# Gate products written to PSUM in their copy's order, 64 first products ahead, eight rows' dot products at the seam

## The chip, the cores and the metric

The kernel runs on 1 core of one Trainium2 chip, as one launch. The metric is the device time of that launch in microseconds (us). TensorE is called PE here, its weight loads PEld, VectorE DVE, ScalarE ACT, GpSimd POOL, and SyncE SP.

## The reference

Three transformer-like layers over 512 tokens of width 1024, in float32. The part that the change touches most is the mixture with 16384 experts in the first layer:

```python
q = (nf @ w_q).reshape(t, PEER_HEADS, D_KEY)
...
v1, i1 = lax.top_k(s1, TOPK)
v2, i2 = lax.top_k(s2, TOPK)
cand = (v1[..., :, None] + v2[..., None, :]).reshape(t, PEER_HEADS, TOPK * TOPK)
vals, ci = lax.top_k(cand, TOPK)
...
idx = (e1 * N_KEYS + e2).reshape(t, PEER_HEADS * TOPK)
gates = jax.nn.softmax(vals.astype(jnp.float32), axis=-1).astype(n.dtype)
...
ug = expert_u[ib]
act = jax.nn.gelu(jnp.einsum("td,tkd->tk", xb, ug)) * gb
vg = expert_v[ib]
return jnp.einsum("tk,tkd->td", act, vg)
```

Each token takes 8 heads x 16 experts. Ahead of it stands a mixing layer (gated convolutions with a normalization per head, spatial gating), behind it a state-space layer, an attention layer and two feed-forward layers, each with normalizations and matrix products.

## The kernel before

Activations lie feature by partition, 8 tiles of 128 x 512. A weight matrix is read in strips of 128 output features; every strip (`wr`) is split into a rounded part `wh` (ACT) and a remainder `wl` (DVE, or POOL where the strip's `pool` flag is set), and each product is three matmuls for each 128 inputs: `wh` by the rounded activation, `wl` by it, `wh` by its remainder (lines 161 to 163). `lin` is one strip's product. `lin2` takes the first two strips behind a normalization together: all but the last input tile of the one, then of the other, then the last tile of both.

The code writes every engine's instructions in the order in which that engine runs them. Small steps of a chain (a normalization, a convolution) are put into a heap by `later(n, f)` and come out n products later; a list `bg` of background steps with costs is drawn from after each product, by a credit.

The experts are done in two ways. The first 128 tokens gather their experts' rows, which are multiplied and summed on DVE and POOL's queue (`first_block`: a row's dot product is line 980, its gather line 977). The other 384 tokens go dense: for each of 128 groups e of 128 experts a first product (`u`, 24 matmuls of 384 columns), a Gelu, a multiplication with the gates `G`, and 18 matmuls of 512 columns into six PSUM banks (`pv`, line 1112).

The gates stage comes ahead of the dense stage. `plan_choice` finds the 16 best candidates of a token and head, ending in `ints` and `trans`: `trans` turns expert numbers and gates with three PE transposes (`pt`, lines 867 to 869). `plan_gates` makes from them a gate for every token and expert: `front` builds one-hot tables for 8 tokens (`oh2` and `oh1`, then `gh`, four of the eight on ACT, line 906, four on DVE, line 908), `mid` multiplies them on PE (`pg`, line 917, four tokens to a PSUM bank), and `back` copies each bank on ACT into `gb` (line 924), which goes to DRAM (`gd`) and comes back in the dense stage as `G`. `gb` holds, for each of 128 experts, 32 tokens side by side:

```python
pg = self.px_((P, 4, P), "pg")
...
    nc.tensor.matmul(pg[:, t % 4, :], oh2[:, t, :], gh[:, t, :], start=True, stop=True)
...
copy(gb[:, c % 2, :, o : o + 4].rearrange("p e t -> p t e"), pg)
```

While this goes on, PE runs first products of groups that need no gates yet: `R` = 56 of the 128 are done ahead, their Gelus are kept in DRAM (`sd`), and the dense stage reads them back. `bg` also holds 32 early rows' dot products (`EARLY`) of the first 128 tokens. The costs of `bg` are spread evenly over the first products of this stage.

## Time and profile before

| what | value |
|---|---|
| median of 3 runs | 3077.76 us (3073.26 to 3085.12) |
| profiled execution, its own time | 3078.27 us |
| span of the profiled execution | 3076.5 us |
| mean granted TensorE clock | 0.971 |
| PE busy | 2908.9 us, 95% |
| DVE busy | 2218.9 us, 72% |
| ACT busy | 1303.4 us, 42% |
| POOL busy | 1093.8 us, 36% |

The time is that of the launch, and the span runs from its first to its last instruction. Busy matmuls overlap at their ends, so that a busy PE is not a PE at its peak. The granted clock is a share of full speed; 1.0 is 2.4 GHz and the lower level is 1.2 GHz, and a share between is a stretch that had both.

### The profile page before, as it was taken

Reading aid. Unit: us, or ns where it says so; the run is one execution under the profiler, and the core shown is the slowest. Engines: PE = TensorE matmul, PEld = TensorE weight load, DVE = VectorE, ACT = ScalarE, POOL = GpSimd, SP = SyncE. Lnnn points to the kernel's source line nnn. Section 1 sums busy time; section 2 is a strip of 40 time slices with the busy share of each in tenths; the row PEclk is TensorE's granted clock in tenths of the full one; section 3 lists DMA queues with packets and bytes.
Section 4 is the critical chain, followed back from the end, with each engine's and each line's share of the span. In section 5 each row is a group of like instructions: output and inputs, shape, how many; then the busy total and the mean of one; then the engine's idle time right before and its main releaser. Section 6 shows DMA issues by size and latency. Waiting matters only on the chain. (4 is left out here: it accounts for less than half of the span.)

```text
span 3076.5 us, 39413 instructions
## 1 busy us (share of the span) xinstructions
PE 2908.9 (95%) x14359; PEld 2445.6 (79%) x14359; DVE 2218.9 (72%) x3788; ACT 1303.4 (42%) x2209; POOL 1093.8 (36%) x936
## 2 busy tenths in 40 slices
PE   8999988889999999999999979999999998999998
PEld 6677888788887888888787768888877766888886
DVE  7945888986888889988886674666666356566665
ACT  4333246566433433443335343433344345433333
POOL 3224566653248778877872321000011011100001
PEclk9889999899999999999999989999999989999999
DMA  4124335679778988898894473233332211333323
GB/s 140 48 83 148 97 129 186 232 245 313 252 263 313 336 318 322 331 350 315 312 328 147 125 225 103 77 102 99 99 97 95 77 42 42 96 103 96 96 72 99
DMA packets 235067, 534.77 MB, mean 174 GB/s; under 512 B 35135, under 2 KB 127683, under 8 KB 222202
## 3 DMA queue, kind: packets, MB, share of 16 engines
q1 hardware_dynamic: 170570, 343.69, 33.9%
q0 software_dynamic: 24832, 140.74, 12.4%
q10 hardware_dynamic: 39472, 47.84, 4.5%
q8 instruction: 113, 1.85, 0.2%
q14 instruction: 80, 0.66, 0.1%
HBM read 468.75 MB, written 63.44 MB: 173 GB/s over the span
## 5 line engine op out<-in xcount | busy, mean ns | idle before, releaser
L150 DVE TENSOR_TENSOR wl<-wr,wh 128x1024 fp32r<-128x1024 f32 (+2 forms) x453 | 545.3, 1213 | 510.1 <-ACT wh L148 509.9
L148 ACT ACTIVATE wh<-wr 128x1024 fp32r<-128x1024 f32 (+2 forms) x552 | 544.7, 995 | 403.7 <-PE mm L163 196.2
L161 PE MATMUL mm<-xn,wh 128*128 128x512 f32 x1296 | 520.9, 402 | 14.3 <-ACT xn L119 8.9
L163 PE MATMUL mm<-xn,wh 128*128 128x512 f32 x1296 | 512.4, 395 | 5.8 <-DVE xn L114 5.8
L162 PE MATMUL mm<-xn,wl 128*128 128x512 f32 x1296 | 512.1, 395 | 1.9 <-POOL wl L150 1.9
L230 POOL TENSOR_TENSOR accs<-accs,sq 128x512 f32<-128x512 f32 x56 | 86.3, 1541 | 1042.7 <-ACT sq L229 1038.4
L1112 PE MATMUL pv<-wh,A 128*128 128x512 f32 x1536 | 437.5, 397 | 15.8 <-ACT A L117 5.9
L150 POOL TENSOR_TENSOR wl<-wr,wh 128x1024 fp32r<-128x1024 f32 x99 | 241.3, 2439 | 449.1 <-ACT wh L148 446.6
L161 PE MATMUL mm<-n,wh 128*128 128x384 f32 x1024 | 350.6, 342 | 0.8 <-ACT gs L705 0.8
L162 PE MATMUL mm<-n,wl 128*128 128x384 f32 x1024 | 345.6, 337 | 5.9 <-DVE wl L150 4.3
L1112 PEld LDWEIGHTS pv<-wh,A 128*128 128x128 f32 x1536 | 286.8, 189 | 80.6 <-DVE A L112 11.0
L163 PE MATMUL mm<-n,wh 128*128 128x384 f32 x1024 | 345.9, 338 | 3.1 <-DVE n L114 3.1
L161 PEld LDWEIGHTS mm<-xn,wh 128*128 128x128 f32 x1296 | 248.5, 192 | 69.3 <-ACT xn L119 8.9
L163 PEld LDWEIGHTS mm<-xn,wh 128*128 128x128 f32 x1296 | 247.7, 191 | 61.4 <-DVE xn L114 8.3
L162 PEld LDWEIGHTS mm<-xn,wl 128*128 128x128 f32 x1296 | 248.4, 192 | 55.2 <-POOL wl L150 2.3
L1112 PE MATMUL pv<-wl,A 128*128 128x512 f32 x768 | 241.9, 396 | 9.4 <-DVE wl L150 9.3
L117 ACT ACTIVATE A<-ga 128x384 fp32r<-128x384 f32 x128 | 67.3, 526 | 357.7 <-DVE ga L1076 357.7
L162 PEld LDWEIGHTS mm<-n,wl 128*128 128x128 f32 x1024 | 194.2, 190 | 9.7 <-DVE wl L150 5.6
L161 PEld LDWEIGHTS mm<-n,wh 128*128 128x128 f32 x1024 | 194.5, 190 | 4.9 <-issue 1.4
L163 PEld LDWEIGHTS mm<-n,wh 128*128 128x128 f32 x1024 | 194.0, 189 | 3.4 <-DVE n L114 3.4
L1112 PEld LDWEIGHTS pv<-wl,A 128*128 128x128 f32 x768 | 144.0, 189 | 49.0 <-DVE wl L150 17.3
L1670 ACT ACTIVATE uc<-up,vec 128x512 f32<-128x512 f32 x88 | 71.8, 816 | 203.8 <-DVE up L1668 203.8
(414 smaller groups left out, 5438.9 us busy)
## 6 DMA issues: line engine op xcount, KB each, us to landing
wr<-in_exp_u SPq DMA_DIRECT2D x128, 512.0 KB, 5.4
wr<-in_exp_v SPq DMA_DIRECT2D x128, 512.0 KB, 6.9
wr<-in_w_up SPq DMA_DIRECT2D x88, 512.0 KB, 3.6
gd<-gb ACTq DMA_DIRECT2D x48, 512.0 KB, 5.0
G<-gd SPq DMA_DIRECT2D x32, 768.0 KB, 6.3
wr<-in_w_dn SPq DMA_DIRECT2D x64, 320.0 KB, 2.9
wr<-in_w_pg SPq DMA_DIRECT2D x24, 512.0 KB, 4.2
sd<-gs SPq DMA_DIRECT2D x56, 192.0 KB, 2.9
```

Source lines behind the costliest of these rows:

```text
L117: nc.scalar.activation(hi, src, AF.Copy)
L148: nc.scalar.activation(s.hi, s.raw, AF.Copy)
L150: eng.tensor_tensor(s.lo, s.raw, s.hi.bitcast(F32), ALU.subtract)
L161: t.matmul(ps, wh, xh, start=start, stop=False)
L162: t.matmul(ps, wl, xh, start=False, stop=False)
L163: t.matmul(ps, wh, xl, start=False, stop=stop)
L230: self.later(1, lambda: nc.gpsimd.tensor_tensor(acc, acc, sq, ALU.add))
L1112: nc.tensor.matmul(pv[2 * b + h], a[:, x, o], w[:, h * T : h * T + T], start=(e == 0 and i == 0 and w is s.hi), stop=last)
L1670: nc.scalar.activation(c, u, AF.Identity, scale=w(2), bias=cb[:, m : m + 1])
```

## The change

- The gate products' PSUM tile is laid out expert by token (`P, P, 4`): each product writes every fourth element, and the copy reads the bank straight and writes runs of four elements. `oh1` is laid out token by token, and DVE's `gh` compares with the copy of the iota that lies in PSUM (`iotaP`).
- `R` goes from 56 to 64: eight more first products run in the gates stage, eight fewer in the dense stage.
- `TAIL`: the last 8 of the 32 early rows' dot products are taken out of the mix and put behind the last gate copy.
- `trans` is drawn from `bg` a few steps after `ints`; the other steps of a block of tokens are spread over one product fewer.
- The dense stage's Gelu writes back into its PSUM bank, and the gate multiplication reads it there.
- `lin2` always goes back and forth between its two strips.
- In the mixing layer, two steps of the head normalization come out a product later.
- The attention bias's small loads are issued earlier, and a negation goes from POOL to DVE.

```diff
-        if first:
-            for k in range(n + 1):
-                for i, j in ((0, k), (1, k - 2)):
-                    if 0 <= j < n - 1:
-                        self.prod(pss[i], ss[i], rhs, j, j + 1)
-        else:
-            for s, ps in zip(ss, pss):
-                self.prod(ps, s, rhs, 0, n - 1)
+        for k in range(n + 1):
+            for i, j in ((0, k), (1, k - 2)):
+                if 0 <= j < n - 1:
+                    self.prod(pss[i], ss[i], rhs, j, j + 1)
...
-            self.later(1, lambda: self.two_rms(d["sq"], self.sel2, 1.0, scale))
+            self.later(1, lambda: self.two_rms(d["sq"], self.sel2, 1.0, scale, 2))
...
-        self.later(1, turn)
+        self.later(lag, turn)
...
-                    self.later(1, lambda: self.head_ln(acc, lambda yn: ln_a(j, yn)))
+                    self.later(2, lambda: self.head_ln(acc, lambda yn: ln_a(j, yn)))
...
-    R = 56
+    R = 64
...
+    TAIL = 8
...
-        self.bg = self.bias_prep() + [(0.1, lambda: nc.scalar.copy(iotaP, iota))]
+        bias, loads = self.bias_prep()
+        loads()
+
+        self.bg = [(0.1, lambda: nc.scalar.copy(iotaP, iota))] + bias
...
-                oh1 = self.loc((P, P, A), BF16, tag="oh1", bufs=2)
+                oh1 = self.loc((P, A, P), BF16, tag="oh1", bufs=2)
...
-                    nc.scalar.activation(gh[:, t, :], oh1[:, :, t], AF.Copy, scale=g)
+                    nc.scalar.activation(gh[:, t, :], oh1[:, t, :], AF.Copy, scale=g)
                 else:
-                    nc.vector.tensor_scalar(out=gh[:, t, :], in0=iota, scalar1=e1, scalar2=g, op0=ALU.is_equal, op1=ALU.mult)
+                    nc.vector.tensor_scalar(out=gh[:, t, :], in0=iotaP, scalar1=e1, scalar2=g, op0=ALU.is_equal, op1=ALU.mult)
...
-                pg = self.px_((P, 4, P), "pg")
+                pg = self.px_((P, P, 4), "pg")
...
-                    nc.tensor.matmul(pg[:, t % 4, :], oh2[:, t, :], gh[:, t, :], start=True, stop=True)
+                    nc.tensor.matmul(pg[:, :, t % 4], oh2[:, t, :], gh[:, t, :], start=True, stop=True)
...
-                copy(gb[:, c % 2, :, o : o + 4].rearrange("p e t -> p t e"), pg)
+                copy(gb[:, c % 2, :, o : o + 4], pg)
...
-        bg = part(1, 1)
...
+        turn = {0: part(1, 1), 1: nxt[1], 2: nxt[2]}
+        turn = {b: (x, x.pop())[1] for b, x in turn.items()}
+        bg = part(1, 1)[:-1] + nxt[1][:3] + [turn[0]]
+        nxt[1] = nxt[1][3:]
...
+        rows, last = rows[: self.EARLY - self.TAIL], rows[self.EARLY - self.TAIL :]
...
-                m = -(-len(more) // (k - j))
+                m = -(-len(more) // max(1, k - 1 - j))
...
-        bg += [(0.0, lambda: mid(n - 1)), (0.0, lambda: back(n - 2)), (0.0, lambda: back(n - 1)), (0.0, rest)]
+            if b in turn:
+                bg.append(turn[b])
+        bg += [(0.0, lambda: mid(n - 1)), (0.0, lambda: back(n - 2)), (0.0, lambda: back(n - 1)), (0.0, rest)] + last
...
-                s = self.tmp((P, TD), tag="gs")
-                nc.scalar.activation(s, ps, AF.Gelu_apprx_tanh)
-                gated(e, s)
+                nc.scalar.activation(ps, ps, AF.Gelu_apprx_tanh)
+                gated(e, ps)
...
-            nc.gpsimd.tensor_scalar(out=rb[0:32, :], in0=rb[0:32, :], scalar1=-1.0, scalar2=None, op0=ALU.mult)
...
+        def negate():
+            nc.vector.tensor_scalar(out=rb[0:32, :], in0=rb[0:32, :], scalar1=-1.0, scalar2=None, op0=ALU.mult)
```

Where the gates stage meets the dense stage, these rows stood on DVE: the last two of 32 dot products (`x,first`, line 980) between the last one-hot tables, then the remainders (`wl`) of the strips that come next, and then the first gate multiplication (`ga`).

```order
L980 SCALAR_TENSOR_TENSOR x,first<-x,accs 128x1024
L894 TENSOR_TENSOR oh_1085_6364<-e2T_2397,held_1484 128x1024
L902 TENSOR_TENSOR oh_1087_6367<-e1T_2396,held_1484 128x512
L908 TENSOR_SCALAR gh_6366<-iota_1482,e1T_2396,gT_2398 128x128 x4
L980 SCALAR_TENSOR_TENSOR x,first<-x,accs 128x1024
L150 TENSOR_TENSOR wl_6410<-wr_6258,wh_6409 128x1024
L150 TENSOR_TENSOR wl_6484<-wr_6319,wh_6483 128x1024
L150 TENSOR_TENSOR wl_6515<-wr_6413,wh_6514 128x1024
L1076 TENSOR_TENSOR ga_6547<-gs_6545,G_6475 128x384
L112 TENSOR_TENSOR A_6549<-ga_6547,A_6549 128x384
```

With the change the last table is followed by all of the last eight dot products (now line 989, five and three), with one remainder between them, and then by the same remainders and the first gate multiplication, which now reads the Gelu from its product's own tile.

```order
L902 TENSOR_TENSOR oh_1117_6559<-e1T_2396,held_1484 128x512
L908 TENSOR_SCALAR gh_6558<-held_1484,e1T_2396,gT_2398 128x128 x4
L989 SCALAR_TENSOR_TENSOR x,first<-x,accs 128x1024 x5
L150 TENSOR_TENSOR wl_6645<-wr_6512,wh_6644 128x1024
L989 SCALAR_TENSOR_TENSOR x,first<-x,accs 128x1024 x3
L150 TENSOR_TENSOR wl_6682<-wr_6606,wh_6681 128x1024
L150 TENSOR_TENSOR wl_6756<-wr_6648,wh_6755 128x1024
L150 TENSOR_TENSOR wl_6789<-wr_6685,wh_6788 128x1024
L1085 TENSOR_TENSOR ga_6820<-mm_6761,G_6747 128x384
L112 TENSOR_TENSOR A_6822<-ga_6820,A_6822 128x384
L150 TENSOR_TENSOR wl_6826<-wr_6759,wh_6825 128x1024
```

On DVE, eight dot products have thus moved from between the tables to behind the last of them and in front of the first `ga`. On PE, in the mixing layer, this is where the second convolution's accumulator (`cacc`) enters its head normalization: behind two `psb` products, which end the two chains before it, and right ahead of a projection's strip (`mm`, of which the last and the first matmul stand here).

```order
L163 MATMUL mm_766<-xn_103,wh_626 128x512
L381 MATMUL psb_791<-rT_737,selT 128x512
L381 MATMUL psb_796<-rT_744,selT 128x512
L339 MATMUL pmn_810<-cacc_460,bd_87 128x512
L161 MATMUL mm_825<-xn_103,wh_701 128x512
```

With the change it stands one strip later, behind a transpose of a chain's statistics (`pst`).

```order
L163 MATMUL mm_805<-xn_103,wh_682 128x512
L370 MATMUL pst_830<-ident,rl_112_729 4x128 x4
L335 MATMUL pmn_837<-cacc_460,bd_87 128x512
L377 MATMUL psb_839<-rT_782,selT 128x512
L357 MATMUL psv_844<-sel_91,sq_785 128x2 x4
```

The `pmn` product has moved past the 24 matmuls of one strip, and the `psv` and `pst` steps of the chains with it.

## Rows read from the trace of the kernel before

**Rows 1.** The page's first part: busy time, share of the span and instructions, by engine.
```profile
PE 2908.9 (95%) x14359; PEld 2445.6 (79%) x14359; DVE 2218.9 (72%) x3788; ACT 1303.4 (42%) x2209; POOL 1093.8 (36%) x936
```
**Rows 2.** Gates stage, dense stage: us, busy PE, PEld, DVE, ACT, POOL, clock, DMA share, GB/s.
```profile
395.00:761.50 366.50, 313.04 (x1953) 305.54 (x1951) 314.52 (x726) 231.13 (x407) 210.17 (x159) 0.94 0.63 216
761.50:1651.00 889.50, 860.04 (x4164) 740.93 (x4165) 754.26 (x956) 349.13 (x629) 598.53 (x572) 0.99 0.86 309
```
**Rows 3.** PE's waits over the span: us in total, times, longest.
```profile
PE pg L917 <- ACT gb L924: 30.9, 20, 6.3
PE pt L867 <- DVE ef L863: 10.2, 2, 6.4
PE pv L1112 <- DVE wl L150: 9.3, 14, 1.5
...
PE pmn L339 <- DVE cacc L442: 6.2, 1, 6.2
...
PE mm L163 <- DVE xn L114: 5.8, 5, 2.4
PE pt L867 <- ACT gb L924: 5.7, 1, 5.7
...
PE pg L917 <- DVE cv L771: 4.2, 1, 4.2
PE pst L374 <- DVE rl L369: 4.1, 2, 3.8
...
PE pb L1761 <- DMA rboh<-in_c_buckets: 3.3, 1, 3.3
```
**Rows 4.** Groups by shape, 395 to 761.5 us: busy us, mean ns, idle before.
```profile
L150 POOL TENSOR_TENSOR wl<-wr,wh 128x1024 fp32r<-128x1024 f32 x45 | 109.5, 2433 | 101.8 <-ACT wh L148 101.6
L917 PE MATMUL pg<-gh,oh 128*128 128x128 f32 x768 | 104.2, 294 | 35.1 <-ACT gb L924 30.9 <-DVE cv L771 4.2
...
L924 ACT COPY gb<-pg 128x512 f32<-128x512 f32 x96 | 94.8, 1092 | 0.1
L908 DVE TENSOR_SCALAR gh<-iota,e1T,gT 128x128 f32<-128x128 f32 x192 | 83.7, 498 | 0.0
...
L980 DVE SCALAR_TENSOR_TENSOR x<-x,accs 128x1024 f32<-128x1024 f32 x32 | 44.4, 1389 | 5.4 <-DMA x<-in_rows_uv,two 5.4
```
**Rows 5.** PE in order of time: eight gate products, then the seam (start, us).
```profile
481.41 1.95 PE L917 MATMUL pg<-gh,oh 128*128 128x128 f32 x16
...
763.33 0.73 PE L1112 MATMUL pv<-wh,A 128*128 128x512 f32 x2 [1.91 <-ACT A L117]
...
767.56 0.33 PE L161 MATMUL mm<-n,wh 128*128 128x384 f32 x1
...
771.57 0.34 PE L163 MATMUL mm<-n,wh 128*128 128x384 f32 x1
775.92 1.22 PE L1112 MATMUL pv<-wh,A 128*128 128x512 f32 x2 [4.01 <-ACT A L117]
```
**Rows 6.** Groups by shape over the span: ACT, as rows 4.
```profile
L376 ACT CAST rT<-pst 4x512 fp32r<-4x512 f32 x22 | 12.5, 573 | 86.9 <-PE pst L374 86.9
...
L1578 ACT COPY y<-yy 64x256 f32<-64x256 f32 x32 | 10.2, 367 | 8.2 <-PE yy L1569 8.0
...
L1593 ACT ACTIVATE yg<-y 128x512 f32<-128x512 f32 x8 | 9.3, 1161 | 22.7 <-DVE y L1589 22.7
...
L1123 ACT COPY gx<-pv 128x512 f32<-128x512 f32 x3 | 1.8, 586 | 1.6 <-PE pv L1112 1.6
```
**Rows 7.** Groups by shape over the span: DVE, as rows 4.
```profile
L1076 DVE TENSOR_TENSOR ga<-gs,G 128x384 f32<-128x384 f32 x128 | 96.2, 751 | 4.5 <-DMA G<-gd 2.5 <-ACT gs L1086 1.9
...
L894 DVE TENSOR_TENSOR oh<-e2T,held 128x1024 f32<-128x1024 f32 x48 | 58.1, 1211 | 14.0 <-PE pg L917 9.4 <-ACT e2T L872 4.6
...
L902 DVE TENSOR_TENSOR oh<-e1T,held 128x512 bf16<-128x512 f32 x48 | 32.5, 678 | 0.0
```
**Rows 8.** One line's instructions, 908: ns min/median/max.
```profile
L908 DVE TENSOR_SCALAR gh<-iota,e1T,gT x192: 328/339/2489, 417.0 to 743.7; 128x128 f32<-128x128 f32 x192
```

More of the change, by code (lines that the diff above doesn't have):

```diff
@@ L181, in prod, with lin2 @@
             self.mm3(ps, s.hi[:, c], s.lo[:, c], *rhs[k], k == 0, k == len(rhs) - 1)
-    def lin2(self, rhs, *posts, first=False):
+    def lin2(self, rhs, *posts):
         n = len(rhs)
@@ L353, in head_ln, with two_rms @@
         mean()
-    def two_rms(self, sq, sel, scale, out):
+    def two_rms(self, sq, sel, scale, out, lag=1):
         nc = self.nc
@@ L526, in mix_in @@
         o = self.W_IN_ORDER
-        self.lin2(xn, posts[o[0]], posts[o[1]], first=True)
+        self.lin2(xn, posts[o[0]], posts[o[1]])
         for m in o[2:]:
@@ L899, in front @@
             if A:
-                oh1 = self.loc((P, P, A), BF16, tag="oh1", bufs=2)
-                sh1 = [P, P, A]
-                nc.vector.tensor_tensor(oh1, e1T[:, t0 : t0 + A].unsqueeze(1).to_broadcast(sh1), iotaP.unsqueeze(2).to_broadcast(sh1), ALU.is_equal)
+                oh1 = self.loc((P, A, P), BF16, tag="oh1", bufs=2)
+                sh1 = [P, A, P]
+                nc.vector.tensor_tensor(oh1, e1T[:, t0 : t0 + A].unsqueeze(2).to_broadcast(sh1), iotaP.unsqueeze(1).to_broadcast(sh1), ALU.is_equal)
             for t in range(HT):
@@ L1750, in loads @@
         def loads():
+            nc.gpsimd.dma_start(oh, I["c_buckets"])
+            nc.gpsimd.dma_start(lq, I["lam"])
             nc.gpsimd.memset(rb, 1e30)
             nc.gpsimd.dma_start(rb[0:32, :], I["rel_bias"])
-            nc.gpsimd.tensor_scalar(out=rb[0:32, :], in0=rb[0:32, :], scalar1=-1.0, scalar2=None, op0=ALU.mult)
-            nc.gpsimd.dma_start(oh, I["c_buckets"])
-            nc.gpsimd.dma_start(lq, I["lam"])
+        def negate():
+            nc.vector.tensor_scalar(out=rb[0:32, :], in0=rb[0:32, :], scalar1=-1.0, scalar2=None, op0=ALU.mult)
         def head(h):
@@ L1772, in lam @@
             nc.vector.tensor_scalar(out=self.nlam, in0=self.nlam, scalar1=-self.LAM_INIT, scalar2=None, op0=ALU.add)
-        return [(0.1, loads)] + [(0.1, lambda h=h: head(h)) for h in range(8)] + [(0.1, lam)]
+        return [(0.1, negate)] + [(0.1, lambda h=h: head(h)) for h in range(8)] + [(0.1, lam)], loads
     def head_rms(self, y, gain, then):
```

## The prediction

> **What bounds the kernel now.** The first view is the page's list of busy times: PE is busy for 2908.9 of 3076.5 us, 95%, the next is DVE with 72% [rows 1]. So the end is set by PE's work, and a change can win only by taking PE's waits away, by a faster clock, or by filling PE's waits with work that PE would do later anyway. This change removes no matmul, so its gain has to come from waits and clock. The second view is busy time by stage [rows 2], which tells where the waits are: PE idles 366.5 - 313.0 = 53.5 us in the gates stage, at a granted clock of 0.94, and 889.5 - 860.0 = 29.5 us in the dense stage, at 0.99. In the gates stage DVE is as busy as PE, 314.5 us, ACT 231.1, POOL 210.2, DMA 0.63. The third view, PE's waits by what ended them [rows 3], names the causes: the gate products wait 30.9 us for the bank copies on ACT and 4.2 us behind DVE's choice, the three transposes of `trans` 10.2 us for DVE's `ef` and 5.7 us for ACT, which is 51.0 of the 53.5. In the mixing layer one product waits 6.2 us for the convolution, and transposes wait 4.1 us for a reciprocal's chain.
>
> **The eight first products that move.** One first product is 24 matmuls. From the first matmul's start at 767.56 to the last one's at 771.57 are 23 steps, 0.1743 us each [rows 5], so eight products are 8 x 24 x 0.1743 = 33.5 us of PE that leave the dense stage. Does the dense stage get shorter by all of it? It has other busy resources: DVE 754.3 of 889.5 us and DMA 0.86 [rows 2], and PE there waits for DVE's remainders (9.3 us [rows 3]). At 856 us the DMA share would be 0.86 x 889.5 / 856 = 0.89 with the same bytes (eight strips of 512 KB less, eight `sd` reads of 192 KB more), and DVE would be at 754 / 856 = 0.88 before what it saves. It saves eight remainders, which now go to POOL in the gates stage, and the multiplications by the gates that read a Gelu in PSUM: with both inputs in SBUF they take 751 ns on average; with one in PSUM a DVE operation takes 678 ns for 512 elements and 1211 for 1024 [rows 7], 1.04 ns an element, so 545 ns for 384 by the same line, and 64 x 0.2 = 13 us. Both stay under 0.9, so I take 26 of the 33.5 us and leave 7.5 to waits that get longer. Bounds: -33.5 (PE's alone), and -10 (DVE or DMA hold most of it back).
>
> **The gates stage.** It takes in the 33.5 us: 313.0 + 33.5 = 346.5 of PE. What of the 53.5 us of waits goes away?
> - `trans` now stands some steps behind `ints`, with other choice steps and a product between: the 15.9 us fall to about 3.
> - The copies. A copy into `gb` takes 1092 ns where a straight copy of the same size takes 586, and the other ACT operation that writes single elements at a stride takes 1161; one that writes runs of 16 elements takes 367 ns for 256, no more than straight [rows 4, 6]. Runs of four are not in the trace: bounds 586 and 1092, and I take 600, since it is the reading and writing of runs that is near the second row. That is 96 x 0.49 = 47 us of ACT's 231.
> - `gh` on DVE takes 498 ns on average but 339 in the median, and up to 2489 [rows 4, 8]; `oh1` and `oh2`, which read PSUM beside the same busy POOL, keep to the line above. From PSUM 128 elements would take 678 - 384 x 1.04 = 279 ns by that line. I take the median, 339, and 192 x 0.16 = 30 us as the most; overlap of neighbours halves it: 15 us of DVE, bounds 0 and 30.
> - The background work is spread over eight products more, so DVE, now 314.5 - 15 = 300 us, is no longer level with PE.
> With that the 35.1 us of waits of the gate products fall to about 12. Waits left: 53.5 - 13 - 23 = 17.5. A PE with fewer gaps has a higher granted clock: 0.94 here, 0.99 in the dense stage [rows 2]. Half of the way, 0.965, takes 346.5 x (1 - 0.94 / 0.965) = 9 us. The stage is then 346.5 + 17.5 - 9 = 355, 12 us less than now. Bounds: no wait falls and no clock is won, 346.5 + 53.5 = 400 (+33.5); all waits fall at a clock of 0.99, 346.5 x 0.94 / 0.99 = 329 (-37.5). Eight more remainders on POOL, 8 x 2.43 = 19 us of a stage in which it is busy for 210 of 366, cost nothing as long as PE finds its strips two products ahead.
>
> **The seam.** The first `pv` waits 1.91 us and the next one 4.01 us for the split gates [rows 5]. After the last gate product stand five first products instead of three, 8.4 us more, in which the gates can go to DRAM and back; this covers both waits, and I take -4. What is late next is the queue on DVE: eight dot products, 8 x 1.39 = 11 us [rows 4], stand ahead of two remainders of late first products, two of the first `pv` strips and the first `ga`, and each from the fourth on needs a gather into one of four slots. Five products are 21 us, so 11 us are covered; gathers that come late by 10 us would not be. Bounds -6 and +8.
>
> **The mixing layer.** The `pmn` product moves past a strip of 24 matmuls of 512 columns, 24 x 512 x 0.454 ns = 5.6 us by the columns of [rows 5], so of its 6.2 us [rows 3] about 0.6 is left, and the 3.8 us of the longest `pst` wait go too: -9. At the layer's end the last `pst` now stands behind the two strips that covered its way to `psb`: a copy of 573 ns [rows 6] and its hand-overs lie open, +3. Together -6, bounds -10 and +3.
>
> **The small edits.** `lin2` in alternating order lets the first strip's later tiles come later: the 5.8 us of waits for the normalized input [rows 3] stand at such places, of which those for the last tile stay: -2. The bias loads: 3.3 us of PE [rows 3], -2. Bounds together -8 and +2; if the second strip's remainder comes too late for its earlier start, that is the +2. The Gelu's new place costs PE nothing, since 18 `pv` matmuls stand between a first product and the need for its gates; with that cover gone it would be the multiplication's own change, 0.2 us less for each of 64. `oh1` turned over keeps its count of elements, and hides behind PE's first products like all of DVE's tables; if not, its 678 ns [rows 7] count 48 times, changed by what no row shows.
>
> **Sum.** -26 - 12 - 4 - 6 - 4 = -52, against the profiled execution's 3078.3 (its span is 3076.5, the rest lies around it; the median of the runs is 3077.8, the same within their spread): 3026 us. A measurement tells about half a per cent, 15 us, from no change.
>
> **The rule against it.** The gate products now write every fourth word of a PSUM bank. No row shows a PE product that writes at a stride. What rows show is that these products have room: eight of them, 16 records, take 1.95 us, 0.122 us for 128 columns or 0.95 ns a column, while the first products take 0.1743 / 384 = 0.454 ns a column [rows 5]. So a write that took two of the fast columns would still be hidden, 128 x 2 x 0.454 = 116 ns; one that took four would make 232 ns of 122, and 768 x 0.11 = 85 us of PE in the gates stage, where PE is already the longest. The Trainium skill, PSUM — Partial Sum Buffer, Specifications (TRN2), speaks against the change: lines are 8 bytes, and an access that is not contiguous slows matmuls significantly; it gives no size, so by it the sum could come out anywhere between hidden and this rival. For the copy, the Trainium skill, SBUF — State Buffer, Specifications (TRN2), has lines of 16 bytes that give full bandwidth from two hits a line on; by it runs of four fp32 would take the straight copy's 586 ns, and the sum would stay as it is to within 2 us.
>
> **The rivals.**
> 1. *Strided writes take PE's time* (the other side): at four fast columns a column the gates stage is 346.5 + 85 + 15 = 447, +80, and the others give -40: 3118 us, slower. It turns slower from +40 us in the stage, near three columns. Against it: the products' half pace. Chance 7%.
> 2. *The moved products don't fill the waits*: PE, ACT and DVE run in written order and wait for each other around four banks, so the waits stay and the stage grows by most of the 33.5. Then +33.5 - 26 - 4 - 6 - 4 = -7, 3071 us, no change. For it: in 366 us neither PE nor DVE was ever the only limit. Against it: the causes named in rows 3 are each touched. Chance 13%.
> 3. *The dense stage doesn't give its part back* (-10, DMA and DVE) and the dot products hold DVE at the seam (+5): -10 - 12 + 5 - 6 - 4 = -27, 3051 us, still faster. For it: DMA at 0.86. Chance 17%.
> The forecast has 63%.
>
> **Range and chances.** The forecast's own range is 3005 to 3048. With rival 3 and half of rival 2 it is 3000 to 3068; left out are rival 1, half of rival 2, and some 6% below. Faster by more than 0.5% (under 3062): forecast and rival 3, 80%. Within: rival 2 and a little, 13%. Slower: 7%.
>
> **What would show it.** In the gates stage: copies near 600 ns (right) or still near 1.1 us; gate products still 1.95 us for 16 records (rival 1 if over 2.5); PE's waits for copies under 15 us and for `ef` near none; its length near 355 us, against 400 for rival 2. The dense stage should last about 860 us; 880 is rival 3. `gh` should have no durations of 2 us. In the mixing layer no wait of 6 us. The prediction is wrong if a new wait, for gathers at the seam or for POOL's remainders, takes the place of those removed.

## The result, and the profile after

The changed kernel takes 3041.22 us (median of 4 runs, 3036.60 to 3042.29) against 3075.51 us before (median of 4, 3070.24 to 3085.12): a ratio of 0.9871, 95% interval 0.9847 to 0.9896, so it is faster by 1.0 to 1.5%. The forecast was 3026 us, in a range from 3000 to 3068. The direction and the range hold; the time is 15 us above the forecast, and this section and the experiments show which terms made that.

The profiled execution took 3036.60 us, with a span of 3034.5 us against 3076.5: 42.0 us less. It is the fastest of its four; by the medians the gain is 34 us. The page's busy times, in the order of [rows 1]:

```profile
PE 2894.9 (95%) x14359; PEld 2435.3 (80%) x14359; DVE 2189.5 (72%) x3781; ACT 1260.6 (42%) x2209; POOL 1109.2 (37%) x943
```

Busy time by stage, with the columns of [rows 2]; the stages are the gates stage and the dense stage:

```profile
385.00:741.10 356.10, 331.31 (x2142) 326.03 (x2141) 303.38 (x722) 198.26 (x424) 229.02 (x166) 0.99 0.70 239
741.10:1618.10 877.00, 838.85 (x3985) 717.34 (x3984) 737.41 (x949) 339.75 (x615) 595.84 (x573) 0.97 0.87 310
```

In the gates stage PE now has 24.8 us without work where it had 53.5, at a clock of 0.99 for 0.94. In the dense stage it has 38.2 us where it had 29.5, and the clock fell from 0.99 to 0.97. PE's waits over the span show both sides of this (columns as in [rows 3]):

```profile
PE pv L1120 <- DVE wl L150: 14.0, 14, 5.8
PE pv L1120 <- ACT A L117: 9.5, 1, 9.5
PE pv L1120 <- ACT wh L148: 9.2, 5, 4.8
PE pg L918 <- ACT gb L925: 8.4, 8, 1.8
...
PE pmn L335 <- DVE vv L413: 7.1, 2, 6.2
...
PE pv L1120 <- DVE A L112: 5.1, 6, 1.8
```

The wait of the gate products for the copies went from 30.9 to 8.4 us. What the list has instead is one wait of 9.5 us of an output product (`pv`) for its split gates, `pv` waits for strips that are longer than before, and a wait of 6.2 us for `vv` in the mixing layer.

The operations that were resized, in the views of [rows 4, 5, 8]: copies and `gh` by line (min/median/max ns), gate products grouped by shape, and eight of them in order of time:

```profile
L925 ACT COPY gb<-pg x96: 560/578/609, 429.4 to 716.0; 128x512 f32<-128x512 f32 x96
```
```profile
L908 DVE TENSOR_SCALAR gh<-held,e1T,gT x192: 391/400/407, 408.7 to 712.9; 128x128 f32<-128x128 f32 x192
```
```profile
L918 PE MATMUL pg<-gh,oh 128*128 128x128 f32 x768 | 93.7, 276 | 8.4 <-ACT gb L925 8.4
```
```profile
486.43 1.95 PE L918 MATMUL pg<-gh,oh 128*128 128x128 f32 x16
```

The copy fell from 1092 to 576 ns on average, and 16 gate product records still take 1.95 us, to the hundredth what they took before, though they now write every fourth word of a bank.

### The profile page after: what moved, and what is told of

The parts are those of the page before. It is cut to its first block, busy times and chain, and to the rows that moved or that the text cites. A ratio compares the mean times of both kernels' runs of the same rounds, so it can differ in the third digit from the quotient of the medians.

```text
span 3034.5 us, 39466 instructions
## 1 busy us (share of the span) xinstructions
PE 2894.9 (95%) x14359; PEld 2435.3 (80%) x14359; DVE 2189.5 (72%) x3781; ACT 1260.6 (42%) x2209; POOL 1109.2 (37%) x943
## 5 line engine op out<-in xcount | busy, mean ns | idle before, releaser
L150 DVE TENSOR_TENSOR wl<-wr,wh 128x1024 fp32r<-128x1024 f32 (+2 forms) x445 | 538.5, 1220 | 497.9 <-ACT wh L148 497.5
L150 POOL TENSOR_TENSOR wl<-wr,wh 128x1024 fp32r<-128x1024 f32 x107 | 261.2, 2443 | 447.0 <-ACT wh L148 440.5
```

What stands on the lines that cost most here:

```text
L150: eng.tensor_tensor(s.lo, s.raw, s.hi.bitcast(F32), ALU.subtract)
```

## The stages side by side

The lengths below are differences of four start times on PE in each profiled run: the last product with `mix` (end of the mixing layer), the last score product, the first `pv`, the last `pv`. "Before the experts" is the span up to the first of them, "queries" from the first to the second, and so on; "rest" ends with the last matmul. The bounds differ a little from those of [rows 2].

| kernel | median us | before the experts | queries | gates | dense | rest |
|---|---|---|---|---|---|---|
| before | 3075.5 | 224.8 | 160.7 | 377.8 | 890.1 | 1416.4 |
| after | 3041.2 | 224.9 | 150.0 | 366.2 | 876.5 | 1410.2 |
| `r56` | 3051.8 | 225.2 | 149.9 | 367.7 | 886.0 | 1406.5 |
| `tail0` | 3041.5 | 226.9 | 151.4 | 369.9 | 876.8 | 1413.0 |
| `before_r64` | 3080.9 | 222.3 | 160.7 | 387.5 | 889.2 | 1417.7 |
| `gate_old` | 3061.6 | 225.4 | 151.5 | 391.8 | 875.0 | 1413.6 |
| `no_gather` | 3023.1 | 225.6 | 150.0 | 365.9 | 860.0 | 1413.2 |
| `short_dot` | 3015.6 | 223.9 | 149.9 | 366.2 | 843.6 | 1412.4 |
| `slow24` | 3047.8 | 222.9 | 149.9 | 367.3 | 886.1 | 1413.0 |
| `mix_old` | 3039.6 | 226.2 | 149.9 | 368.6 | 880.7 | 1415.0 |
| `load_old` | 3046.4 | 223.5 | 156.9 | 368.5 | 877.2 | 1413.6 |
| `split16` | 3034.8 | 225.9 | 151.4 | 367.8 | 869.6 | 1410.9 |
| `spread` | 3030.9 | 223.8 | 150.0 | 367.6 | 869.8 | 1411.5 |

(`split24` is told with its experiment.) The code ahead of the experts is the same in all rows except `before`, `before_r64` and `mix_old`, and still that part spreads from 222.9 to 226.9 us. The dense stage has the same code in `after`, `tail0`, `gate_old`, `mix_old` and `load_old` and spreads from 875.0 to 880.7 us; the rest spreads from 1406.5 to 1415.0 in the rows that have the changed kernel's code. So a difference of 2 us in a single stage tells nothing, nor does one below some 6 us in the dense stage or below some 8 us in the rest. Each row's stages are those of one execution: `r56` and `short_dot` show the fastest of their four runs, 8 and 11 us below their medians, `tail0` and `mix_old` the slowest, 7 and 10 us above.

## The experiments

Two theories stood at the start. **Theory 1**: the dense stage can give back nearly the whole 33.5 us of the eight first products, and what is missing is lost at the seam. **Theory 2**: the dense stage is held by DMA or DVE all along, so that a product taken out turns into waiting.

**`r56`: the eight products moved back.**

```diff
-    R = 64
+    R = 56
```

> The changed kernel (3041 us) with 56 first products ahead, as before. Its dense stage gave back 13.6 us for eight products of 33.5 us. Theory 1 (the dense stage can give nearly all of it back; what is missing is lost at the seam and after it): the dense stage grows by 22 to 33 us over 877, the gates stage shrinks by 12 to 25 from 356, total 3045 to 3058. Theory 2 (the dense stage is held by DMA and DVE all along, so a product less in it is worth 1.7 us and not 4.2): the dense stage grows by some 14 us, the gates stage shrinks by 15 to 30, total 3025 to 3040, faster than the changed kernel.

Measured: 3051.84 us (4 runs, 3043.85 to 3052.16), ratio to before 0.9922 [0.9895, 0.9949]; with them it is 0.9871 [0.9847, 0.9896]. The medians are 10.6 us apart, and the intervals just touch. The total is in theory 1's range, but not for its reason: the dense stage is only 9.5 us longer, less than theory 2 had, and the gates stage does not get shorter at all, 367.7 against 366.2, which neither had. Its row tells why (columns of [rows 2], the gates stage with its bounds in the table, then the first 75 us of the dense stage and the rest of it):

```profile
375.17:742.86 367.69, 323.23 (x2010) 318.29 (x2010) 319.98 (x764) 190.48 (x412) 219.60 (x161) 0.93 0.65 228
```
```profile
742.90:817.90 75.00, 74.92 (x361) 65.48 (x360) 59.36 (x144) 33.10 (x45) 16.04 (x10) 1.00 0.73 259
817.90:1628.90 811.00, 785.56 (x3816) 677.31 (x3815) 689.06 (x814) 318.37 (x585) 581.01 (x561) 0.99 0.87 313
```

With 56 products PE has no work for 44.5 us of the gates stage, and its clock is 0.93; DVE is nearly as busy as PE, 320 of 368 us. The eight products went into these waits, and the clock rose to 0.99: they were free there. That DVE sets the stage's length is likely from this row, but no run took its work away there (`gate_old`, below, adds to it). The same cut through the changed kernel:

```profile
741.10:816.10 75.00, 65.51 (x309) 57.11 (x309) 51.91 (x128) 30.52 (x41) 15.16 (x10) 0.93 0.69 249
816.10:1617.70 801.60, 772.93 (x3676) 660.13 (x3675) 685.49 (x822) 309.17 (x573) 580.68 (x563) 0.98 0.88 316
```

In the first 75 us PE works all the time at full clock with 56 products and 65.5 us at 0.93 with 64. The two timelines of PE at the first `pv` (start, us, instruction, wait) show what happens; with 64:

```profile
744.75 0.62 PE L1120 MATMUL pv<-wh,A 128*128 128x512 f32 x2
754.85 1.22 PE L1120 MATMUL pv<-wh,A 128*128 128x512 f32 x2 [9.49 <-ACT A L117]
```

and with 56:

```profile
746.52 0.62 PE L1120 MATMUL pv<-wh,A 128*128 128x512 f32 x2
746.98 0.33 PE L161 MATMUL mm<-n,wh 128*128 128x384 f32 x1
...
751.00 0.34 PE L163 MATMUL mm<-n,wh 128*128 128x384 f32 x1
751.17 0.62 PE L1120 MATMUL pv<-wh,A 128*128 128x512 f32 x2
```

`ahead` gives the experts 2, 4, 6, 8 for 56 products and 2, 3, 5, 7 for 64. With expert 3 done ahead, no first product stands between the output products of experts 0 and 1, and the `u` strip that comes next is that of expert 4. DVE's and ACT's rows at this place in the changed kernel:

```profile
751.02 1.23 DVE L150 TENSOR_TENSOR wl<-wr,wh 128x1024 fp32r<-128x1024 f32 x1 [10.23 <-ACT wh L148]
752.17 0.55 DVE L1085 TENSOR_TENSOR ga<-gs,G 128x384 f32<-128x384 f32 x1
753.69 0.56 DVE L1085 TENSOR_TENSOR ga<-mm,G 128x384 f32<-128x384 f32 x1 [0.97 <-ACT mm L1094]
```
```profile
749.94 1.06 ACT L148 ACTIVATE wh<-wr 128x1024 fp32r<-128x1024 f32 x1 [9.73 <-DMA wr<-in_exp_u]
```
```profile
733.57 3.13 SPq L135 DMA_DIRECT2D wr<-in_exp_u  x1
```

On ACT and DVE the `wh` and `wl` of a `u` strip stand ahead of the Gelu and the gates of expert 1, and the strip comes at 749.9 us. A `u` strip was issued at 733.57 us and another at 740.77, while the DMA engines were busy to the full with strips, gate reads and the gathers of the last rows (the last but one column, from 716 to 741 us):

```profile
716.00:741.00 25.00, 21.09 (x120) 20.45 (x119) 12.26 (x18) 8.16 (x12) 12.23 (x9) 1.00 1.02 356
```

In `r56` a `u` strip was issued at 719.87 us already. The price of this one wait is more than 9.5 us, since the clock falls behind it: the two `pv` after it take 1.22 us where two took 0.62, and the 18 of expert 1 take 5.6 us where those of expert 0 took 4.1. What the seam costs in all is seen by cutting the dense stage at the first `pv` of expert 4, up to the first `pv` of the last expert (columns of [rows 2]; the kernel before, `r56`, the changed kernel):

```profile
763.33:794.09 30.76, 26.75 (x121) 23.06 (x121) 16.31 (x33) 14.94 (x21) 2.61 (x2) 0.94 0.71 256
794.09:1649.74 855.65, 832.03 (x4039) 716.82 (x4038) 737.36 (x922) 332.66 (x607) 595.75 (x569) 0.99 0.86 310
```
```profile
742.86:768.21 25.35, 25.27 (x122) 21.74 (x121) 14.88 (x32) 14.11 (x20) 2.11 (x2) 1.00 0.68 253
768.21:1625.22 857.01, 831.57 (x4039) 718.07 (x4038) 731.21 (x923) 335.13 (x608) 594.94 (x570) 0.99 0.86 310
```
```profile
741.09:777.01 35.92, 26.43 (x121) 22.77 (x121) 17.51 (x44) 14.19 (x20) 5.30 (x4) 0.86 0.68 253
777.01:1613.95 836.94, 808.27 (x3847) 691.39 (x3847) 717.48 (x903) 323.27 (x591) 590.55 (x569) 0.98 0.87 312
```

Up to expert 4 all three do the same work on PE, 72 output matmuls and two first products of 24 (the counts take in those at the bounds). The changed kernel takes 35.9 us for it, `r56` 25.4 and the kernel before, with its own two waits, 30.8: the seam costs 10.6 us against `r56` and 5.2 against the kernel before. All eight products, 192 matmuls, are missing behind expert 4. There 20.1 of their 33.5 us come back against `r56`, and 18.7 against the kernel before; 20.1 - 10.6 = 9.5. Of the 13.4 us that don't come back against `r56`, PE's waits are only 3.2 (25.4 to 28.7 us); the other 10.2 are in its busy time, which falls by 23.3 us, at a clock of 0.98 for 0.99.

**`tail0`: no row kept for the seam.**

```diff
-    TAIL = 8
+    TAIL = 0
```

> The changed kernel with no row's dot product kept for the seam: all 32 stand between the gate products, as before. Theory 1 (the late gathers of the eight rows, the queues of DVE and GpSimd behind them and the low clock after it cost the dense stage some 12 us): the wait of 9.5 us of the second output product goes, the dense stage is 865 to 870 us, the gates stage grows by 0 to 5, total 3029 to 3037. Theory 2 (DMA and DVE hold the dense stage all along): what the first products of the dense stage win is lost later, the dense stage stays at 874 to 878 and the total is 3039 to 3046.

Measured: 3041.48 us (3038.53 to 3048.09), ratio 0.9885 [0.9857, 0.9912], the changed kernel's time. The dense stage is 876.8, so theory 1 falls in the form that it had here: the eight rows are not what makes the seam late. The wait only moved, to both of the first two output products, since two first products and not five now stand behind the last gate product:

```profile
748.23 1.22 PE L1120 MATMUL pv<-wh,A 128*128 128x512 f32 x2 [4.65 <-ACT A L117]
...
760.73 1.22 PE L1120 MATMUL pv<-wh,A 128*128 128x512 f32 x2 [5.33 <-ACT A L117]
```

Every kernel here with 64 products has such a wait for `A` at its second `pv`, of 5.3 to 9.7 us, with the rows kept or not and in either layout; `r56` has none, and the kernel before, with the product between, waits 4.01 us [rows 5]. That it is the missing product between them, and not something else that differs between 56 and 64, rests on the timelines; a kernel with 64 products of which expert 3 is not one was not run.

**`before_r64`: the eight products alone.** The kernel before, with R = 64.

> The kernel before (3075.5 us) with 64 first products ahead in place of 56 and nothing else. If the room for them comes from the layouts and the order of the gates stage: its waits stay, it grows by 25 to 33 us from 368, the dense stage gives 14 to 26 back, total 3075 to 3095. If eight products fit into the waits without any other edit: the gates stage grows by under 10, total 3055 to 3065.

Measured: 3080.87 us (10 runs, 3069.79 to 3086.87), ratio 1.0008 [0.9993, 1.0023]. The total is as the first expectation had it, but both sizes are smaller: the gates stage grows by 9.7 us, as the second had it, since most of the 33.5 us fits into the waits even with the old layouts, and the dense stage gives back 0.9. By itself the move is worth nothing. From expert 4 on it gives back 5.3 us, 855.7 to 850.4, where the changed kernel gives 18.7:

```profile
805.69:1656.05 850.36, 810.04 (x3848) 687.68 (x3847) 726.63 (x903) 322.49 (x591) 583.84 (x569) 0.98 0.86 307
```

The only edit of the change in the dense stage's own code is the Gelu in its bank, which makes 64 gate multiplications of 740 ns into ones of 547. By itself it brings nothing there either: `r56` has it, and takes 857.0 us. So the dense stage's gain likely needs both, the products moved and this work off DVE; no run took the Gelu's edit alone with 64 products.

**`gate_old`: the old layouts with the new order.**

```diff
-    oh1 = self.loc((P, A, P), BF16, tag="oh1", bufs=2)
+    oh1 = self.loc((P, P, A), BF16, tag="oh1", bufs=2)
...
-    nc.vector.tensor_scalar(out=gh[:, t, :], in0=iotaP, scalar1=e1, scalar2=g, op0=ALU.is_equal, op1=ALU.mult)
+    nc.vector.tensor_scalar(out=gh[:, t, :], in0=iota, scalar1=e1, scalar2=g, op0=ALU.is_equal, op1=ALU.mult)
...
-    pg = self.px_((P, P, 4), "pg")
+    pg = self.px_((P, 4, P), "pg")
...
-    copy(gb[:, c % 2, :, o : o + 4], pg)
+    copy(gb[:, c % 2, :, o : o + 4].rearrange("p e t -> p t e"), pg)
```

> The changed kernel with the layouts of the gates stage as before: gate products into a bank row by row and a strided copy of 1.1 us, one-hot of the first half strided, the other half from the iota in SBUF. The order of the steps and the 64 first products stay. If the layouts make the room for the eight products: the gates stage grows by 20 to 35 us from 356, total 3061 to 3076. If the order of the steps does it: by under 8, total 3041 to 3049.

Measured: 3061.60 us (10 runs, 3055.11 to 3069.85), ratio 0.9947 [0.9931, 0.9963]: 20 us above the changed kernel, and the gates stage is 25.6 us longer. The layouts make the room: in its gates stage DVE is busy for 332.7 us, 21 more than in the changed kernel's, and ACT for 246.0, 44 more. Which of the three edited operations counts most was not tried apart. Its groups, as in [rows 4]:

```profile
L908 DVE TENSOR_SCALAR gh<-iota,e1T,gT 128x128 f32<-128x128 f32 x192 | 97.8, 572 | 0.0
L918 PE MATMUL pg<-gh,oh 128*128 128x128 f32 x768 | 97.6, 282 | 16.0 <-ACT gb L925 16.0
L925 ACT COPY gb<-pg 128x512 f32<-128x512 f32 x96 | 95.6, 1106 | 0.0
```

The copy costs 1106 ns again, and DVE's `gh` 572 on average; PE's gate products take 282 ns, no less than with the strided writes.

**`no_gather` and `short_dot`: what holds the rest of the dense stage.** The first leaves out the gathers from the 38th row on (and scales the products of these rows, which are made in place again and again):

```diff
     def fetch(j):
+        if j >= E + self.SLOTS:
+            return
```

The second shortens the dense stage's dot products to 128 of 1024 columns:

```diff
-    dot(j, slot(j)[:, 0 : 8 * P])
+    u = slot(j)[:, 0:P]
+    nc.vector.scalar_tensor_tensor(out=u, in0=u, scalar=1.0, in1=nt[:, 0:P], op0=ALU.mult, op1=ALU.mult, accum_out=s[:, j : j + 1])
```

> The changed kernel (3041 us) without the gathers of the rows from the 38th on (92 of 128, 1 MB each), so some 92 MB of the dense stage's 272 are not moved; the dot products and sums of those rows work on what the slots hold. The output is not the reference's. Theory A (the transfers' rate holds the dense stage, so a first product taken out of it turns into waiting for strips): the DMA share falls from 0.87 to about 0.6, the waits for `wh` and `wl` go, the dense stage falls from 876 to 835 to 850, total 2998 to 3018. Theory B (VectorE's queue of dot products, remainders and gates holds it): the dense stage stays at 868 to 880, total 3033 to 3045. Theory C (the engine itself and its clock, whatever comes in): 868 to 880 as well, with clock and waits unchanged.

> The changed kernel with the 96 dot products of the dense stage over 128 columns in place of 1024, about 1.2 us less each, 115 us less of VectorE's 737 in that stage. The output is not the reference's. Theory B (VectorE's queue holds the dense stage): its waits for `wl` and for `A` go, the dense stage falls from 876 to 840 to 858, total 3005 to 3025. Theory A (the transfers): the dense stage stays at 870 to 880, total 3035 to 3045.

Measured: 3023.13 us (3020.77 to 3026.85) without the gathers, 3015.63 (3004.82 to 3024.61) with short dot products. Dense stages 860.0 and 843.6. The busy times of the dense stage in each, first without the gathers:

```profile
741.50:1601.50 860.00, 824.49 (x3984) 710.77 (x3983) 734.89 (x949) 339.34 (x614) 507.96 (x482) 0.99 0.61 205
```
```profile
740.10:1583.70 843.60, 822.09 (x3984) 711.59 (x3983) 643.83 (x949) 341.87 (x614) 536.82 (x573) 0.99 0.88 322
```

Theory B holds best: with 94 us less on DVE the stage is 33 us shorter at the same DMA share (by the medians the kernel gains 26), PE's idle time falls from 38.2 to 21.5 us (9.7 of it the seam's wait), and its busy time by 17 us at a clock of 0.99. Theory A is not excluded, but the transfers are the smaller part: with a third of the bytes gone (share 0.87 to 0.61) the stage is 16.5 us shorter, between the ranges of the theories, half of what A had and more than B had. These gathers also leave POOL, which is busy for 508 us in place of 596. PE's waits for `wl` even rise:

```profile
PE pv L1122 <- DVE wl L150: 22.7, 16, 5.7
PE pv L1122 <- ACT A L117: 9.5, 1, 9.5
```

Its idle time stays at 35.5 us and only the clock is better. Why the clock is, with waits of the same sum, stays open. So DVE's work is the larger part of what holds the stage. In its written order a dot product of 1.4 us and a sum of 1.35 us stand ahead of the `wl` or the `A` that PE needs next; whether it is these lumps, the next four runs ask.

**`slow24`, `split16`, `split24` and `spread`: the order of that queue.** `slow24` puts more of the rows' work beside experts that still have a first product:

```diff
-    SLOW = 1.6
+    SLOW = 2.4
```

`split16` cuts each row's step into its sum and its dot product, which are drawn from `bg` apart; `split24` has this cut and the rate of 2.4:

```diff
-    items = [(1.2 if j < E or j >= P else 2.4, lambda j=j: step(j)) for j in range(P + 2)]
+    items = []
+    for j in range(P + 2):
+        if E <= j < P:
+            items += [(1.2, lambda j=j: step(j, 0)), (1.2, lambda j=j: step(j, 1))]
+        else:
+            items.append((1.2, lambda j=j: step(j)))
```

`spread` has the cut, a rate of 1.2, and draws half of an expert's items between its two strips and half behind them:

```diff
     unit_u(e + L)
+    self.run_bg(rates[e] / 2)
...
-    self.run_bg(rates[e])
+    self.run_bg(rates[e] / 2)
```

> The changed kernel with 2.4 in place of 1.6 as the rate of gather work beside an expert whose first product is still to be made, so that fewer gathers stand beside the 4.2 us of an expert without one, where strip, gates and gather together ask for about 390 GB/s, and more beside the 8.4 us of the others. Theory A: the transfers are spread more evenly, waits for `wh` and `wl` fall, dense stage 862 to 872, total 3027 to 3037. Theory B: two or three dot products now follow each other on VectorE, its remainders come later, dense stage 878 to 890, total 3043 to 3055. If neither counts: 3038 to 3044.

> The changed kernel (3041 us) with each dense-stage step of a gathered row cut into two items of the same cost sum: the sum over an earlier row with the gather, and the dot product. So one operation of 1.4 us and not two stand together ahead of the next remainder, gate product or split on VectorE; no operation is added or left out. Theory B, in the form that VectorE's queue hurts by its lumps (2.8 us of row work ahead of work that the next expert needs): waits for `wl`, `wh` and `A` fall, dense stage 858 to 870, total 3022 to 3035. If it hurts by its sum alone (737 of 876 us busy, whatever the order): dense stage 872 to 880, total 3036 to 3046.

> The same cut, with 2.4 in place of 1.6 as the rate beside experts whose first product is still to be made. Uncut, this rate made the dense stage 886 us, 9.6 more. An expert of 4.2 us without a first product has 2.87 us of VectorE's own work, one of 8.4 us with it 4.05 us, so by busy share more of the rows' work belongs to the second. If the lumps made the loss of the uncut one: dense stage 855 to 872, total 3020 to 3037, as fast as the cut alone or faster. If the rate itself is wrong: dense stage 880 to 890, total 3043 to 3055.

> The cut of the rows' work into single items, carried on: of each expert's items one half stands between its two strips' products and one half behind them, at a rate of 1.2 (the cut alone at 1.6 took 3034.8 us with a dense stage of 869.6; at 2.4 it was 881.6). If VectorE's lumps hold the dense stage: 858 to 868, total 3024 to 3034. If what can be had from the order is had with the first cut: 868 to 874, total 3033 to 3040. If rows' work in the middle delays the output strip's remainder, which is needed next: 874 to 885, total 3039 to 3050.

Measured: `slow24` 3047.78 us (3047.10 to 3048.90) with a dense stage of 886.1, as theory B had it: waits for `A` from DVE rise from 5.1 to 13.6 us, which is the whole growth of PE's waits there. `split16` 3034.76 (3031.21 to 3035.95), ratio 0.9861 [0.9844, 0.9877], dense stage 869.6, at the upper edge of what was expected if the lumps count. `split24` 3040.72 (3040.36 to 3043.71), dense stage 881.6, as the second expectation had it, the total 2 us under it: the cut wins 4.5 us of that stage against `slow24`, within the spread of equal code, but the rate itself is wrong. `spread` 3030.89 (5 runs, 3025.58 to 3037.95), ratio 0.9847 [0.9823, 0.9870], dense stage 869.8, no shorter than with the cut alone; the total is in the first expectation's range, the stage in the second's. `split16` and `spread` have the two lowest medians of the kernels that compute everything, 6 and 10 us below the changed one; their intervals overlap with its own, so that they beat the kernel before is shown, and that they beat the changed one only likely. For it: no run of `split16` is as slow as the fastest of the changed kernel (3035.95 against 3036.60), and none of `split24` as the fastest of `slow24` (3043.71 against 3047.10).

That it is the lumps that the cut takes away is not shown. `split16` from expert 4 on, and its waits for DVE:

```profile
779.28:1611.13 831.85, 802.47 (x3848) 685.07 (x3847) 720.96 (x903) 323.46 (x591) 597.73 (x569) 0.99 0.87 314
```
```profile
PE pv L1131 <- DVE wl L150: 13.5, 19, 5.9
PE pv L1131 <- DVE A L112: 8.0, 9, 3.6
```

The waits for `wl` and `A` were to fall and are 21.5 us in sum, against 19.1 in the changed kernel. PE is idle for 29.4 us here, against 28.7; the 5.1 us that this stretch is shorter are all in its busy time, at a clock of 0.99 for 0.98.

**`mix_old` and `load_old`: the terms ahead of the gates stage.** The first has the mixing layer's two lags as before:

```diff
-    self.later(1, lambda: self.two_rms(d["sq"], self.sel2, 1.0, scale, 2))
+    self.later(1, lambda: self.two_rms(d["sq"], self.sel2, 1.0, scale, 1))
...
-    self.later(2, lambda: self.head_ln(acc, lambda yn: ln_a(j, yn)))
+    self.later(1, lambda: self.head_ln(acc, lambda yn: ln_a(j, yn)))
```

The second has the bias table's loads as before, in `bg`, with the table of buckets behind the negation on POOL:

```diff
-    bias, loads = self.bias_prep()
-    loads()
-
-    self.bg = [(0.1, lambda: nc.scalar.copy(iotaP, iota))] + bias
+    self.bg = self.bias_prep() + [(0.1, lambda: nc.scalar.copy(iotaP, iota))]
```

> The changed kernel with the two lags in the mixing layer as before (one product earlier). The changed kernel's layer ends where the kernel before ended it (224.89 against 224.81 us), with a wait of 6.2 us for `vv` in place of one of 6.2 us for the convolution. Theory 1 (the lags remove one wait and make the other, so they are worth nothing): the layer ends at 224 to 226, total 3038 to 3045. Theory 2 (the lags win the 6 us that were forecast and something else in the change costs them): the layer ends at 229 to 232, total 3045 to 3051.

> The changed kernel with the loads of the bias table as before: in the background work, the table of buckets after a GpSimd multiplication. If the loads made the 10.7 us by which the stage of the expert queries became shorter (160.7 to 150.0 us from the mixing layer's end to the last score product): that stage is 157 to 161 us and the total 3048 to 3053. If they are worth the 2 us of the forecast: 152 to 153, total 3042 to 3045, and the alternating order of the first two strips or the clock made the rest.

Measured: `mix_old` 3039.55 us (3037.84 to 3049.18), ratio 0.9867 [0.9850, 0.9883]; its layer ends at 226.2, inside the spread of the same code. The lags are worth nothing that can be told. Its waits there are those of before, the two that the lags took away:

```profile
PE pmn L335 <- DVE cacc L438: 6.2, 1, 6.2
PE pst L370 <- DVE rl L365: 4.1, 2, 3.7
```

`load_old` 3046.42 us (3044.40 to 3048.96), ratio 0.9899 [0.9883, 0.9916]. The query stage is 156.9 us, 6.9 more than with the early loads and just under the first expectation, though PE waits only 3.0 us for the table. Two windows of it, the second right behind the wait (columns of [rows 2]):

```profile
223.50:238.00 14.50, 11.48 (x56) 9.60 (x54) 3.67 (x4) 3.74 (x5) 10.47 (x12) 0.97 0.50 164
238.00:253.00 15.00, 15.00 (x56) 11.03 (x57) 2.44 (x8) 5.88 (x12) 7.60 (x6) 0.80 0.49 145
```

In the 15 us behind the wait the granted clock is 0.80, a mean of its two levels of 2.4 and 1.2 GHz. In the changed kernel no wait stands there and the clock is 1.00 in the same place. So the 3.0 us cost another 3 in clock: 56 PE instructions in these 15 us where the changed kernel makes 70. The last of the 6.9 us is a later wait for `n`, 3.1 us against 1.9.

## Why the forecast was right in sign and 15 us off

| term | forecast | profile |
|---|---|---|
| gates stage | -12 (-37.5 to +33.5) | -11.6 |
| dense stage and seam | -26 and -4 (-33.5 to -10, -6 to +8) | -13.6: -18.7 from expert 4 on, +5.2 ahead of it |
| mixing layer | -6 (-10 to +3) | +0.1 |
| small edits | -4 (-8 to +2) | -10.7 (queries) and -6.2 (rest) |
| sum | -52 | -42.0 |

**The gates stage** is right as a sum, and its steps nearly so: PE's idle time fell from 53.5 to 24.8 us, not to 17.5; the clock went to 0.99 and not to 0.965, so that PE is busy for 331.3 us of its window where 346.5 less 9 were reckoned. The forecast charged the stage 33.5 us and took 45 off again, 36 of it for waits that the other edits were to remove. With all these edits and 56 products (`r56`) PE is still idle for 44.5 us, 11 less than before within the same bounds; the products fill another 20. So a simpler account fits better: the other engines' chain sets the stage's length, with DVE the busiest of them, and the products go into PE's gaps. That the sum agrees to 0.4 us is in part luck. Copies near 600 ns (576), waits for copies under 15 us (8.4), `ef` near none (2.4), a length near 355 (356.1), and in the dense stage a multiplication with the Gelu in PSUM of 545 ns (547, where [rows 7] had 751) came as said. `gh` lost its 2 us outliers but takes 400 ns, not 339; the mean still fell by 98 ns.

**Rival 1** (strided writes take PE's time) is out: 1.95 us for 16 records before and after, and 276 ns a product against 282 with straight writes. The Trainium skill, PSUM — Partial Sum Buffer, Specifications (TRN2), has non-contiguous access slow matmuls significantly; no run here shows that for these products of 128 columns with a 16-byte stride, and the measurement decides. **Rival 2** (the moved products don't fill the waits) is out by `r56`; what comes nearest to it is `before_r64`, where the old layouts leave no gain.

**The dense stage and the seam** are the terms that were mis-sized. The step that failed at the seam is "this covers both waits, and I take -4": it counted the first products behind the last gate product, which cover the first `pv`, and missed that the longer list of products ahead takes the one away that stood between the first and the second `pv`. The wait of 4.01 us there became 9.49 us, and up to expert 4 the stage got 5.2 us longer where 4 less were reckoned, a size inside the bounds but for another reason than the dot products that they name (`tail0`). The other step is "I take 26 of the 33.5 us": from expert 4 on 18.7 us came back. DVE's work at 0.84 of the stage was seen, but taken as room; `short_dot` shows that it is not, and `before_r64` that without the Gelu's edit only 5.3 us come back. That it is the lumps in DVE's order that count is argued, not shown. Of **rival 3**, its -10 + 5 for the stage with its seam was nearer to the measured -13.6 than the forecast's -30, and the stage's length of 877.0 us nearer to the 880 that was to show it; DVE and not DMA was the larger cause. Its total of 3051 us lies 10 us above the median, the forecast's 15 below it.

**The mixing layer** gained nothing and came out nearer to its second bound: the 6.2 us for the convolution became 1.1 and the 4.1 us of `pst` 0.3, but a wait of 6.2 us for `vv` took their place, a new wait in the place of the old, which the prediction named only for the seam and for POOL's remainders. The step that failed is the -9 taken from "about 0.6 is left": it followed the one product that moves and not the next chain that the same lag makes late.

**The small edits** were priced by their waits alone. The loads were put at 2 us for a wait of 3.3; with the clock behind it it is worth some 6 to 7, by `load_old`. That leaves 4 of the query stage's 10.7, and the rest's 6.2, to the strips in alternation and to the spread of the runs; that PE's waits for `xn` fell from 5.8 to 0.6 us is seen in the trace, but no run took this edit alone.

**The sum.** The dense stage, the seam and the mixing layer fell short by 22.5 us, the small edits gave 12.9 more than they were given credit for, and so the profiled executions differ by 42.0 where 52 were forecast. The other 5 us of the 15 come from the runs: the profiled execution of the changed kernel is the fastest of its four. So that the total came as near as 15 us is partly luck: the small edits made up for more than half of what the other terms lacked.

## What to carry to other kernels

Where PE is 95% busy, price a wait with the clock behind it: here 3.0 us cost 6 and 9.5 cost 10.9. Before moving work into a stage that has gaps, find which engine sets that stage's length: where it is another than PE, the moved matmuls can be free there, but the stage that they leave gets shorter only as far as its other engines can follow, and a list that is made longer can take away the one item that covered a hand-over. A second engine that is busy for 84% of a stage is not room: 94 us less of DVE's work made the stage 33 us shorter in the profiled execution. Cutting 2.8 us of its background work in two likely took some 5 to 7 us off without removing an instruction, and why is open.

## What the runs showed of the hardware

- A PE product of 128 columns that writes every fourth fp32 word of a PSUM bank takes no longer than one that writes 128 in a row (1.95 us for 16 records in both).
- An ACT copy of 512 fp32 elements that writes runs of four takes 576 ns, and one that writes single elements 1092 to 1106. The Trainium skill, SBUF — State Buffer, Specifications (TRN2), with its lines of 16 bytes, agrees with this step.
- DVE's compare of 128 elements from SBUF beside a busy POOL takes 339 ns in the median and up to 2489; from PSUM it takes 391 to 407, and the mean is lower.
